# A shorter list of warm-up matmuls ahead of a weight-gradient matmul

## Chip, core and metric

The kernel runs on one core of one Trainium2 chip. The metric is device time in microseconds (us), as the median of several executions. Next to these timed runs there is one profiled execution with a trace; its times are counted from the first instruction of its span.

## What is computed

```python
def setup_inputs():
    batch, m, k, n = 16, 512, 1024, 768
    return {
        "input": np.random.randn(batch, m, k).astype(np.float32),
        "grad_output": np.random.randn(batch, m, n).astype(np.float32),
    }

def reference(input, grad_output):
    return np.einsum('bmk,bmn->kn', input, grad_output).astype(np.float32)
```

The batch and m axes are summed over together, so this is one matmul: an X of 8192 x 1024, transposed, times a G of 8192 x 768, which gives 1024 x 768 in fp32. Both inputs come from HBM as fp32 and are multiplied as bf16.

## The kernel before

**Tiles.** The 8192 rows are cut into 32 units of 256 rows. A unit is a pair of tiles, `xp` (128 partitions x 2 x 1024) and `gp` (128 x 2 x 768), in bf16. `LOADS` gives each unit a kind: the first five and the last are "s" (multiplied plainly, as two row tiles of 128), the other 26 are "P". For a "P" unit VectorE (DVE) first makes sums and differences of its quarters into `xe` and `ge` (`sum_x` and `sum_g`, lines 202 to 220), and TensorE then does seven products of quarters in place of eight.

**Loads.** The first row tile's G and the first two row tiles' X come as fp32 (`gf`, `xf`) through the queues of SyncE and ScalarE (lines 150 to 153), and are rounded to bf16 by DVE and ScalarE (ACT) in line 224. Everything else comes through GpSimd's (POOL's) queue, which rounds on the way: lines 180 and 182 for single row tiles, then lines 175 and 176 for whole units, G first and then X. Transfers are issued in this order far ahead of their use; a later one waits for a free buffer of the pool `pairs`.

**Warm-up.** Before the first data is there, TensorE (PE) multiplies constants into one PSUM bank that nobody reads before it is overwritten. The list `WARMUP` (line 88) names these matmuls, and the loop in lines 155 to 164 issues them; the profile puts them at line 158. They read constants of 1.0 that lie in SBUF from the start, so they wait for no load. All the real matmuls have line 328 (`multiply`).

**Order.** `PLAN` (lines 24 to 85) is a list written out by hand: each token is a multiplication of a block for some row tiles, a filling of a bank with a running sum (line 302, ACT), a closing of a bank (lines 355 to 371), a set-aside (383), an adding of what was set aside (392) or a stage of the sums. The order on PE, DVE, ACT and POOL is that of the program and is not rescheduled. So an instruction that waits holds up all that stands behind it on its engine.

**Instructions.** Each real matmul is two instructions on PE, a weight load and a multiplication, and so is each bf16 warm-up matmul. PE's instructions are brought in while the kernel runs, by transfers that use the same 16 DMA engines as the loads; the page lists them as "q8 instruction".

Of the kernel before, what the change touches and what calls it, by code (L numbers as in the profile page):

```python
# [9 lines left out]
P = 128  # L10
# [74 lines left out]
).split()  # L85


WARMUP = [("b", 512)] + [("s", 80)] * 54
PAIRS_HELD = 10
SUMS_HELD = 8  # L90
ASIDE = 24
# [18 lines left out]
def kernel(  # L110
# [6 lines left out]
    nc = tc.nc  # L117
    bf16 = mybir.dt.bfloat16
    f32 = mybir.dt.float32
# [34 lines left out]

    wps = psum.tile([P, 512], f32, name="bank7")
    for dt, cols in WARMUP:
        rows = 32 if dt == "s" else P
        nc.tensor.matmul(
            wps[0:rows, 0:cols],
            nc.const_aps.tensor(1.0, (P, rows), bf16),  # L160
            nc.const_aps.tensor(1.0, (P, cols), bf16),
            start=True,
            stop=True,
        )
# [4 lines left out]
    for u, kind in enumerate(LOADS):  # L169
# [3 lines left out]
        if u >= MERGED:  # L173
            rows = slice(2 * u * P, 2 * (u + 1) * P)
            nc.gpsimd.dma_start(out=gp, in_=G[rows, :].rearrange("(p m) n -> p m n", m=2))  # L175
            nc.gpsimd.dma_start(out=xp, in_=X[rows, :].rearrange("(p m) k -> p m k", m=2))  # L176
        for h in range(2):
            s = 2 * u + h
# [222 lines left out]
    for token in PLAN:  # L401
# [6 lines left out]
        elif op == "f":  # L408
            block, banks = rest.split("@")
            b, _, b2 = banks.partition("+")  # L410
# [9 lines left out]
        else:  # L420
            block, n = token.split(".")
            block, _, banks = block.partition("@")
            b, _, b2 = banks.partition("+")
# [33 lines left out]
```

## Time and profile before

| what | value |
|---|---|
| timed runs | 161.83, 161.84, 162.16 us; median 161.84 |
| profiled execution | span 160.0 us, 1.84 less than that median |
| PE | 155.1 us busy (97%), 1057 matmuls, of which 55 are the warm-up |
| DVE | 146.8 us busy (92%) |
| ACT / POOL | 118.2 us (74%) / 39.6 us (25%) |
| the 16 DMA engines | 33.42 MB in 12447 packets, "9" in nearly all slices up to the 35th of 40 |
| PE's instruction transfers (q8) | 8 packets, 0.13 MB |
| HBM | 58.72 MB read, 3.15 MB written |

"Busy" is an engine's own time with an instruction on it; PEld is the loading of weights, which overlaps multiplication. The page gives no time of the profiled execution besides its span, so what lies around the span is taken as the 1.84 us to the median. A slice is a fortieth of the span, 4 us. A wait is put down to what released it.

### The profile page before, as it was taken

The page shows a single profiled execution, that of the slowest core. Times are in us where ns is not written, and L with a number is a line of the kernel's source. Part 1 is how long each engine was busy: PE and PEld are TensorE (multiplying, and loading weights), DVE is VectorE, ACT ScalarE, POOL GpSimd, SP SyncE. Part 2 cuts the span into 40 slices and gives each one's busy share as a digit, 9 for nine tenths or more (in the row PEclk, how much of TensorE's full clock was granted, in tenths as well). Part 3 has the DMA queues.
Part 4 walks back from the last instruction along what each step waited for, and adds up shares of the span by engine and source line. Part 5 has one row for each costly group of instructions (what it writes and reads, how often), then busy time and mean ns, then how long its engine had stood idle before and what let it go on. Part 6 is the DMA issues. An engine that isn't in the chain of part 4 may idle for free.

```text
span 160.0 us, 3074 instructions
## 1 busy us (share of the span) xinstructions
PE 155.1 (97%) x1057; PEld 98.4 (62%) x1057; DVE 146.8 (92%) x344; ACT 118.2 (74%) x274; POOL 39.6 (25%) x74
## 2 busy tenths in 40 slices
PE   8999899999999999999999999999999999999991
PEld 7666476666666666666656666666666666656661
DVE  0689979999999999999999999999999989998991
ACT  3683444899788788988986596985789855685960
POOL 7442222122221222222122221222222100004510
PEclk9999999999999999999999999999999999999999
DMA  5999999999999999999999999999999999931786
GB/s 174 298 211 215 212 216 213 211 215 212 212 213 213 212 211 213 213 214 214 216 215 213 212 211 214 212 213 210 212 217 212 212 215 215 212 64 45 218 294 234
DMA packets 12447, 33.42 MB, mean 209 GB/s; under 512 B 1424, under 2 KB 4240, under 8 KB 12432
## 3 DMA queue, kind: packets, MB, share of 16 engines
q0 software_dynamic: 9360, 28.64, 90.5%
q1 hardware_dynamic: 2640, 3.41, 6.6%
q10 hardware_dynamic: 432, 1.18, 2.0%
q8 instruction: 8, 0.13, 0.3%
q14 instruction: 7, 0.06, 0.1%
HBM read 58.72 MB, written 3.15 MB: 387 GB/s over the span
## 4 chain that ended last, share of the span: by engine, by line
PE 85%; DMA 8%; POOL 2%; ACT 1%; issue 1%; DVE 1%; ACTq 0%; POOLq 0%
PE bank L328 85%; DMA xp<-in_input_dram 8%; POOL gp L180 1%; POOL xp L182 1%; ACT bank L302 1%; ACT acc L367 1%; DVE acc L369 1%; POOL gp L175 0%; ACT macc L367 0%; ACTq L367 0%; POOLq L441 0%
## 5 line engine op out<-in xcount | busy, mean ns | idle before, releaser
L328 PE MATMUL bank<-gp,xp 128*128 128x384 bf16 (+2 forms) x690 | 109.1, 308 | 0.8 <-DMA xp<-in_input_dram 0.5
L328 PEld LDWEIGHTS <-xp 128*128 128x128 bf16 x690 | 64.6, 98 | 37.9 <-DMA xp<-in_input_dram 0.8
L328 PE MATMUL bank<-ge,xe 128*128 128x384 bf16 x312 | 59.7, 326 | 0.0
L328 PEld LDWEIGHTS <-xe 128*128 128x128 bf16 x312 | 30.3, 98 | 19.0
L302 ACT COPY bank<-macc 128x384 f32<-128x384 f32 x73 | 34.4, 486 | 7.0 <-DVE macc L371 2.5
L367 ACT COPY macc<-bank 128x384 f32<-128x384 f32 x68 | 31.4, 482 | 5.7 <-PE bank L328 5.0
L176 POOL DMA_DIRECT2D xp<-in_input_dram x30 | 15.9, 529 | 53.0 <-DVE ge L218 21.0
L367 ACT COPY acc<-bank 128x384 f32<-128x384 f32 (+1 forms) x39 | 18.3, 477 | 12.3 <-PE bank L328 12.2
L175 POOL DMA_DIRECT2D gp<-in_grad_output_dram x30 | 15.9, 531 | 37.4 <-DMA gp<-in_grad_output_dram 10.4
L371 DVE TENSOR_TENSOR acc<-bank,acc 128x384 f32<-128x384 f32 x45 | 23.7, 555 | 0.6 <-PE bank L328 0.4
L302 ACT COPY bank<-acc 128x384 f32<-128x384 f32 (+2 forms) x45 | 20.9, 480 | 4.3 <-DVE acc L371 1.9
L383 ACT COPY aside<-bank 128x384 f32<-128x384 f32 x43 | 19.1, 483 | 6.0 <-PE bank L328 5.1
L371 DVE TENSOR_TENSOR macc<-bank,macc 128x384 f32<-128x384 f32 x38 | 21.2, 558 | 0.6 <-PE bank L328 0.5
L206 DVE TENSOR_TENSOR xe<-xp 128x1024 bf16<-128x1024 bf16 x26 | 18.0, 692 | 0.0
L392 DVE TENSOR_TENSOR acc<-acc,aside 128x384 f32<-128x384 f32 x26 | 14.5, 556 | 1.3 <-ACT aside L383 1.3
L216 DVE TENSOR_TENSOR ge<-gp 128x768 bf16<-128x768 bf16 x26 | 14.5, 558 | 0.0
L392 DVE TENSOR_TENSOR macc<-macc,aside 128x384 f32<-128x384 f32 x20 | 11.2, 563 | 0.0
L210 DVE TENSOR_TENSOR xp<-xp,xe 128x512 bf16<-128x512 bf16 x26 | 11.0, 425 | 0.1
L208 DVE TENSOR_TENSOR xe<-xe,xp 128x512 bf16<-128x512 bf16 x26 | 11.0, 424 | 0.1
L399 POOL TENSOR_TENSOR acc<-acc,macc 128x384 f32<-128x384 f32 x5 | 5.0, 1000 | 21.6 <-DVE macc L364 19.7
L220 DVE TENSOR_TENSOR gp<-ge,gp 128x384 bf16<-128x384 bf16 x26 | 9.3, 358 | 0.1
L218 DVE TENSOR_TENSOR ge<-gp,ge 128x384 bf16<-128x384 bf16 x26 | 9.3, 359 | 0.0
(20 smaller groups left out, 42.7 us busy)
## 6 DMA issues: line engine op xcount, KB each, us to landing
xp<-in_input_dram POOLq DMA_DIRECT2D x30, 512.0 KB, 16.9
gp<-in_grad_output_dram POOLq DMA_DIRECT2D x30, 384.0 KB, 16.8
out_dram<-acc SPq DMA_DIRECT2D x12, 192.0 KB, 2.0
xf<-in_input_dram ACTq DMA_DIRECT2D x2, 512.0 KB, 5.0
gp<-in_grad_output_dram POOLq DMA_DIRECT2D x3, 192.0 KB, 6.4
out_dram<-acc SPq DMA_DIRECT2D x6, 96.0 KB, 2.2
xp<-in_input_dram POOLq DMA_DIRECT2D x2, 256.0 KB, 7.8
gf<-in_grad_output_dram SPq DMA_DIRECT2D x2, 192.0 KB, 4.4
```

Source lines behind the costliest of these rows:

```text
L175: nc.gpsimd.dma_start(out=gp, in_=G[rows, :].rearrange("(p m) n -> p m n", m=2))
L176: nc.gpsimd.dma_start(out=xp, in_=X[rows, :].rearrange("(p m) k -> p m k", m=2))
L206: nc.vector.tensor_sub(out=xe[:, 0:2, :], in0=x[:, 1::-1, :], in1=x[:, 3::-2, :])
L208: nc.vector.tensor_sub(out=xe[:, 2, :], in0=xe[:, 0, :], in1=x[:, 0, :])
L210: nc.vector.tensor_add(out=x[:, 1, :], in0=x[:, 2, :], in1=xe[:, 2, :])
L216: nc.vector.tensor_add(out=ge[:, 0:2, :], in0=g[:, 0:2, :], in1=g[:, 1::2, :])
L302: nc.scalar.copy(out=tile_[:, t0 : t0 + c1 - c0], in_=sum_of(p, q)[:, c0:c1])
L328: nc.tensor.matmul(tile_[:, t0 : t0 + c1 - c0], stat, mov[:, c0:c1], start=start, stop=True, skip_group_check=True,)
L367: nc.scalar.copy(out=d, in_=b)
L371: nc.vector.tensor_add(out=d, in0=b, in1=d)
L383: copy(out=aside[i], in_=b[:, t0 : t0 + NH])
L392: nc.vector.tensor_add(out=dst, in0=dst, in1=aside[i])
```

## The change

```diff
-WARMUP = [("b", 512)] + [("s", 80)] * 54
+WARMUP = [("b", 512), ("f", 512), ("f", 512), ("b", 512)]
...
     for dt, cols in WARMUP:
-        rows = 32 if dt == "s" else P
+        kind = f32 if dt == "f" else bf16
         nc.tensor.matmul(
-            wps[0:rows, 0:cols],
-            nc.const_aps.tensor(1.0, (P, rows), bf16),
-            nc.const_aps.tensor(1.0, (P, cols), bf16),
+            wps[:, 0:cols],
+            nc.const_aps.tensor(1.0, (P, P), kind),
+            nc.const_aps.tensor(1.0, (P, cols), kind),
```

Before, the warm-up is one bf16 matmul of 128 x 128 weights and 512 columns, and then 54 of 128 x 32 weights and 80 columns. After, it is a bf16 one of 512 columns, two fp32 ones of 512 columns and again a bf16 one, all with 128 x 128 weights. In the program's own list an fp32 matmul is one instruction (it loads its weights itself), so 110 instructions become 6, 104 fewer. In the compiled stream of PE each fp32 matmul is two pairs of a load and a multiplication, one for each of two parts of the weights, so 110 become 12, 98 fewer. On DVE, ACT, POOL and SyncE the instructions and their order stay as they are, and on PE everything behind the warm-up does too.

## The prediction

> **What bounds the kernel now.** First the page, for who is busy and who waits.
>
> ```profile
> span 160.0 us, 3074 instructions
> ...
> PE 155.1 (97%) x1057; PEld 98.4 (62%) x1057; DVE 146.8 (92%) x344; ACT 118.2 (74%) x274; POOL 39.6 (25%) x74
> ...
> L328 PE MATMUL bank<-gp,xp 128*128 128x384 bf16 (+2 forms) x690 | 109.1, 308 | 0.8 <-DMA xp<-in_input_dram 0.5
> ```
>
> TensorE is busy all but 5 us, and all its real matmuls together waited 0.8 us. So only the start, the end and that one wait can move the time through TensorE. Next the chain of work that ended last, in order of time, for where that wait lies.
>
> ```profile
> 4.05 0.48 POOL gp L175
> 4.53 12.36 DMA xp<-in_input_dram
> 16.89 0.05 issue
> 16.93 62.51 PE bank L328 x417
> ...
> 82.28 74.04 PE bank L328 x490
> ```
>
> The columns are start, length and what. Up to 16.89 the end is set by a load, the X of the third unit; from 16.93 on by TensorE, to 156.3. How fast TensorE starts matters only as far as it reaches 16.93 late. Then TensorE's first microseconds in the timeline, and equal stretches of it in the view by windows (stretch; its length; PE's busy time and matmuls; then the other engines, clock, DMA).
>
> ```profile
> 0.78 4.29 PE L158 MATMUL bank<-const-bfloat16-1.0 128*128 128x512 bf16 x55 [0.78 <-PEq L441]
> 5.29 2.98 PE L328 MATMUL bank<-gp,xp 128*128 128x256 bf16 x16 [0.22 <-ACT xp L224]
> ```
>
> ```profile
> 5.30:6.40 1.10, 1.10 (x5) 0.67 (x6) 0.37 (x2) 0.24 (x1) 0.33 (x1) 1.00 1.08 298
> 6.40:7.50 1.10, 1.10 (x10) 0.69 (x8) 1.03 (x5) 1.03 (x3) 0.00 (x0) 1.00 1.16 207
> ...
> 16.45:16.95 0.50, 0.04 (x2) 0.02 (x2) 0.50 (x2) 0.48 (x1) 0.00 (x0) 1.00 1.15 227
> ```
>
> The warm-up ends 0.2 us before the first real matmul, which waits for ACT's rounding. In the 1.1 us before 6.40 TensorE does 5 matmuls, in the 1.1 us after it 10: its clock comes to full pace at 6.40 only. The 1.00 that the page prints before that is not a measurement: the trace's own clock record begins at 6.40. And in the third stretch TensorE stands still. Last, the DMA view around 13 us.
>
> ```profile
> q0 software_dynamic: 62, 0.24, 100.5%
> q8 instruction: 1, 0.02, 4.9%
> ```
>
> Between 13.2 and 14.4 us, while the loads fill all 16 DMA engines, one of them carries a packet of TensorE's instructions: in the packet records 16384 bytes, at 13.33, for 0.945 us. The landing records say what it costs. The awaited X comes in 16 pieces, one for each engine: 15 land between 15.59 and 16.16, and the last at 16.89. The transfer before it has no such straggler (13.14 to 13.69), and all later ones have: unit four's X lands by 20.51 in 15 pieces, the last at 21.20. So **the wait at 16.9 is made by the instruction packet**, which put one engine 0.73 us behind for good, as it is never idle.
>
> **The change part by part.** *Instructions.* The eight q8 packets begin when 215, 504, 722, 986, 1238, 1497, 1747 and 1955 of TensorE's records have started: one for about 249 (1955 less 215, by 7). They go by count. With 98 fewer ahead of them (104 in the program's list), the first comes at the old record 313 to 319, at 21.5 to 21.9 us, less what TensorE has gained: about 21. By then X of units three and four is in. Unit three's X then lands at 16.16 instead of 16.89, and TensorE, 0.04 behind it as now, can go on at 16.20 instead of 16.93: at most **-0.73 us**.
>
> *The warm-up's length.* TensorE is ready for that X at 16.31 now (its last matmul before started at 16.15, and they are 0.163 apart). That is after it lost half of 5.29 to 6.40 to the slow clock, 0.555 us. So the new restart is the later of 16.20 and 16.31 + (new loss - 0.555). A bf16 matmul of 512 columns takes 0.51 (0.78 to 1.29, where the next starts). No row shows an fp32 one. From below: as bf16, 0.51 each, so the warm-up ends at 0.78 + 4 x 0.51 = 2.8. From above: DVE's bf16 add of 1024 columns takes 692 ns and its fp32 add of 384 takes 556, so 0.68 and 1.45 ns a column, 2.14 times; both operands are wide here, so 4.6 times 0.51, 2.35 each, and the end is at 6.5. The compiled stream has two multiplications for each, so I stay near the upper end with 1.9: 0.78 + 0.51 + 3.8 + 0.51 = 5.6. The first real matmul then starts 0.31 late. With the clock at full pace from 6.40 again, the loss is 0.31 + 0.40 = 0.71, TensorE is ready at 16.47, and -0.46 is left. With an end at 5.29 it is -0.62; where the clock comes by 5.8 it is the full -0.73. One execution does not tell where between these the clock falls, so I take **-0.6**. The Trainium skill, "FP8 and Floating Point Precision", TensorE Precision Notes, gives true fp32 four passes through the array; at the slow pace of 0.43 us for 512 columns that would be an estimate of 1.7 each, and the sum would be -0.62.
>
> *What is hidden.* Going 0.6 earlier, TensorE and DVE need every later load 0.6 earlier, and the DMA engines are full until about 140, so those land where they do now. Between landing and use there are now 0.13 us at unit four's X (21.20 to 21.33), but there the straggler goes too: 15 pieces are in by 20.51, the need is at 20.7. After that X is used on TensorE 0.63 us or more after landing (the least at 139.06 and 143.46, with 0.63 and 0.73). On DVE it is 0.59 at 37.3 and 0.46 to 0.52 at 130.5, 134.6 and 138.9, so DVE may stand up to 0.15 there; its own idle gaps of 0.33 at 142.1 and 0.71 at 145.3 take that back. Cost 0; with that cover gone, 0.15. The other instruction packets come some 8 us later too; one that meets the engine furthest behind just ahead of 139 costs up to 0.6. The 0.26 us that TensorE stands at 81.9 for DVE and ACT moves along; should it vanish, that is the low end.
>
> *Sum.* 160.0 - 0.6 = 159.4 of span, and with the 1.84 between this span and the median, **161.24**. Its own range: 161.84 - 0.73 - 0.26 = 160.85 to 161.5.
>
> **The rivals.** *The instruction transfer was hidden, or the wait comes back.* If the straggler has another cause, X still lands at 16.89. Or TensorE's stream asks for its instructions 1 us sooner than I count, and the packet delays unit four's X: it lands at 21.20 again, where TensorE then stands 0.5. Either way 161.7 to 161.84. For it: 0.13 us of margin is little, and the packets' spacing varies from 208 to 289 records. Against: 15 of 16 pieces were early, from the transfer that was on its way at 13.33 on and on none before. The Trainium skill, "Runtime: Kernel Launch", Instruction fetch mechanics, calls the cost of crossing such a 16 KiB block mostly hidden; by that rule nothing would change, but the 0.73 us of the late piece speaks against it.
>
> *The clock comes later.* If the fp32 matmuls end early, or count less for the clock, TensorE runs its real matmuls at half pace for longer. The loss is half of (opening - 5.29). It decides once it is 0.555 + 0.626 = 1.18 (16.93 less 16.31 is the 0.626), so for an opening after 7.65. Before, the clock came 5.62 us after TensorE began; if only real matmuls counted, it would come at 5.29 + 5.62 = 10.9, with a loss of 2.81: ready at 18.57 and 163.5. The middle of 7.65 and 10.9 is 9.3: loss 2.0, +0.82, **162.7**. For it: no row shows an fp32 matmul, and one as quick as bf16 would leave TensorE idle from 2.8 to 5.29. Against: the small matmuls before filled only 32 columns of the array and still opened the clock. The Trainium skill, "TensorE: Matmul & The Clock Gate", HAM clock gate, has the clock decided in free-running windows of 3.41 us; one window late would be 9.81, an estimate of 162.9.
>
> *The warm-up is simply too long.* Past 2.35 us for an fp32 matmul the first real one starts after 6.5; each 0.1 us more costs 0.2. At 2.6 each the end is at 7.0, the loss 1.71, and the time 162.4. Only wider operands than the rows suggest would do that.
>
> **How the numbers follow.** Forecast 0.62, hidden or returned 0.16, clock later 0.17, too long 0.05. Within 0.2% (0.32 us) is what a measurement of this kernel can't tell from no change. Nearly all of the forecast's cases lie beyond it: faster 0.62, same 0.17, slower 0.21. The range goes from 160.8, with the stall at 81.9 gone, to 162.6, which takes in the second case, the third and the near half of the clock's; about 0.1 lies above.
>
> **What would show it.** Right: the first q8 packet near 21 us, and no piece of unit three's X late; TensorE's wait for it gone or under 0.1; TensorE's last matmul 0.5 to 0.7 earlier than 156.4. The fp32 step: the first real matmul between 5.29 and 5.6. Wrong: a full clock later than 7.65 (few matmuls between 6.4 and 7.5), a wait at 21, or a new one at 139.

## The result and the profile after

| | before | after |
|---|---|---|
| timed runs | 161.83 to 162.16, median 161.84 | 162.42 to 162.84, median 162.75 |
| ratio after to before | | 1.0042, 95% interval 1.003 to 1.0054 |
| span of the profiled execution | 160.0 | 161.1 (that execution took 162.84) |
| last matmul on PE starts | 156.43 | 156.08 |
| from there to the end of the span | 3.55 | 4.98 |

The change makes the kernel 0.9 us slower by the medians and 0.7 by the ratio, where 0.6 us faster was forecast. It did bring TensorE forward, though by 0.34 us only; then the end, from the start of TensorE's last matmul on, became 1.43 us longer (4.98 against 3.55). The difference of the two, 1.09, is that of the spans. The profiled execution is the slowest of the change's five (the others have spans of 160.5 to 161.0), so the 1.43 is at the upper end of what was lost, if TensorE gained as much in them.

First the page of the kernel after, the lines that answer to those shown of before.

```profile
span 161.1 us, 2976 instructions
...
PE 155.3 (96%) x1008; PEld 95.8 (59%) x1008; DVE 146.7 (91%) x344; ACT 118.3 (73%) x274; POOL 39.8 (25%) x74
...
L328 PE MATMUL bank<-gp,xp 128*128 128x384 bf16 (+2 forms) x690 | 109.2, 307 | 0.2
```

The engines' work is what it was. In the last line the wait for a load is gone: 0.8 us of idle time has become 0.2, and no load is named as its releaser. Next TensorE's first microseconds in the timeline, and two stretches in the view by windows (the same columns as before).

```profile
0.78 0.58 PE L158 MATMUL bank<-const-bfloat16-1.0 128*128 128x512 bf16 x1 [0.78 <-PEq L441]
1.16 3.62 PE L158 MATMUL bank<-const-float32-1.0 128*128 128x512 f32 x4
4.57 0.63 PE L158 MATMUL bank<-const-bfloat16-1.0 128*128 128x512 bf16 x1
5.22 2.96 PE L328 MATMUL bank<-gp,xp 128*128 128x256 bf16 x18
```

```profile
5.30:6.40 1.10, 1.10 (x9) 0.67 (x10) 0.65 (x3) 0.54 (x2) 0.34 (x1) 1.00 1.10 302
...
16.45:16.95 0.50, 0.39 (x3) 0.12 (x2) 0.50 (x2) 0.35 (x1) 0.50 (x1) 1.00 1.08 215
```

The warm-up ends in time: the first real matmul starts at 5.22, and in the 1.1 us from 5.30 TensorE does 9 matmuls where it did 5 before, so its clock is up earlier (the clock record begins, at full, at 5.48; before at 6.40). At 16.45, where it stood still before, it works 0.39 of 0.50 us. The chain of work that ended last says what holds it up there instead.

```profile
5.22 7.23 PE bank L328 x45
...
13.88 2.88 DVE acc L371 x6
16.76 0.04 issue
16.81 58.25 PE bank L328 x390
...
81.94 74.04 PE bank L328 x490
155.98 0.02 issue
156.00 0.02 ACTq L367
156.02 0.04 issue
156.06 0.38 ACT acc L367
156.44 0.29 DVE acc L369
```

Where the chain before had a load of 12.36 us, it now has a run of six of DVE's additions, until 16.76. The matmul that waited for the load starts at 16.20 (16.93 before), so the whole 0.73 is won there. But then TensorE stands 0.27 us behind the matmul of 16.37 and 0.14 behind that of 16.97, for banks that DVE has still to empty. So the load no longer decides, and DVE does: 0.34 is left of the gain, at 81.94 (82.28 before) as at the end.

The chain stops at the end of DVE's last copy, at 156.73, and says nothing of the 4.3 us behind it, in which the results are stored. These lines are of the DMA view of before, from 144.0 to 145.4 us, and then of after, from 152.3 to 154.3.

```profile
DMA packets 1, 0.02 MB, mean 12 GB/s; under 512 B 0, under 2 KB 0, under 8 KB 0
...
q8 instruction: 1, 0.02, 6.2%
```

```profile
q1 hardware_dynamic: 138, 0.19, 26.8%
q8 instruction: 1, 0.02, 4.5%
```

TensorE's last instruction packet (the eighth) came at 144.20 before, when all loads were in and no store was under way: it was the only packet in 1.4 us. In the kernel after it comes at 152.45, among the output stores (q1). What the stores do around it is in SyncE's timeline (start, time to issue; the eleventh of the 20 stores, before, then after) and in the windows (the last two columns are the DMA engines' busy share and GB/s; before, then after).

```profile
152.69 0.38 SPq L346 DMA_DIRECT2D out_dram<-acc  x1
```

```profile
152.34 1.93 SPq L346 DMA_DIRECT2D out_dram<-acc  x1
```

```profile
152.00:153.00 1.00, 1.00 (x8) 0.60 (x7) 1.00 (x4) 0.80 (x3) 0.67 (x1) 1.00 0.39 140
153.00:154.00 1.00, 1.00 (x8) 0.59 (x6) 1.00 (x3) 1.00 (x3) 0.00 (x0) 1.00 0.90 326
154.00:155.00 1.00, 1.00 (x8) 0.59 (x6) 1.00 (x3) 0.60 (x3) 0.00 (x0) 1.00 0.97 346
155.00:156.00 1.00, 1.00 (x10) 0.76 (x8) 1.00 (x3) 0.00 (x0) 0.00 (x0) 1.00 1.03 369
```

```profile
152.00:153.00 1.00, 1.00 (x8) 0.59 (x6) 1.00 (x4) 0.80 (x3) 0.33 (x1) 1.00 0.35 109
153.00:154.00 1.00, 1.00 (x8) 0.59 (x6) 1.00 (x4) 1.00 (x4) 0.00 (x0) 1.00 0.31 109
154.00:155.00 1.00, 1.00 (x9) 0.60 (x7) 1.00 (x3) 0.26 (x2) 0.00 (x0) 1.00 0.26 91
155.00:156.00 1.00, 1.00 (x12) 0.87 (x11) 0.98 (x2) 0.00 (x0) 0.00 (x0) 1.00 1.03 369
```

The store that meets the packet takes 1.93 us to issue, until 154.27, and until it is done SyncE issues no other. Of the store ahead of it, issued at 151.92, 15 of the 16 pieces are in by 153.77 in the landing records, and the last at 155.24: one engine is behind. The DMA view from 153.5 to 154.5 us says what the others do meanwhile (packets, MB, share of 16 engines; before, then after).

```profile
q1 hardware_dynamic: 270, 0.37, 101.7%
```

```profile
q1 hardware_dynamic: 4, 0.01, 4.1%
```

The 4.1% are less than a sixteenth, the share of one engine at work. So the other 15 stand, until the next store is issued and its packets begin. From 152 to 155 the DMA engines work 0.92 us (0.35 + 0.31 + 0.26) where they worked 2.26 before: 1.34 us of all 16 engines are lost. They can't be made up: from 155 on the stores go at 364 to 369 GB/s in both kernels, one of 192 KB each 0.54 us, nearly to their end. The last store's transfer ends at 158.72 before and at 159.80 after, 1.08 later, as the span does.

### The profile page after: what moved, and what is told of

The parts are those of the page before. It is cut to its first block, busy times and chain, and to the rows that moved or that the text cites. A ratio compares the mean times of both kernels' runs of the same rounds, so it can differ in the third digit from the quotient of the medians.

```text
span 161.1 us, 2976 instructions
## 1 busy us (share of the span) xinstructions
PE 155.3 (96%) x1008; PEld 95.8 (59%) x1008; DVE 146.7 (91%) x344; ACT 118.3 (73%) x274; POOL 39.8 (25%) x74
## 3 DMA queue, kind: packets, MB, share of 16 engines
q1 hardware_dynamic: 2640, 3.41, 6.6%
## 4 chain that ended last, share of the span: by engine, by line
PE 89%; ACT 3%; DVE 3%; issue 1%; ACTq 0%
PE bank L328 87%; PE bank L158 3%; DVE acc L371 2%; ACT bank L302 1%; ACT macc L367 1%; ACT acc L367 1%; DVE acc L369 1%; ACTq L367 0%
## 5 line engine op out<-in xcount | busy, mean ns | idle before, releaser
L371 DVE TENSOR_TENSOR macc<-bank,macc 128x384 f32<-128x384 f32 x38 | 20.9, 551 | 0.6 <-PE bank L328 0.5
```

Of the source, the lines that this page charges most:

```text
L371: nc.vector.tensor_add(out=d, in0=b, in1=d)
```

## The experiments

The theory: the place of the instruction packets decides, both at the loads and at the stores, and that place follows from the number of instructions ahead of them on TensorE. Its rivals: the fp32 warm-up matmuls themselves, or the fullness of SyncE's queue. Each run has another warm-up list, or another queue for some stores, or both. The table gives the PE instructions of the warm-up, when the first and the last packet begin, when X of unit three is complete, when TensorE's last matmul starts, what follows from there to the span's end (the tail), the DMA share from 152 to 155 us, the median, and the ratio to the kernel before on the same chip. The medians are of more than one chip, so kernels are compared by the ratio.

| kernel | instr. | first | X three | last | PE last | tail | share | median | ratio (95%) |
|---|---|---|---|---|---|---|---|---|---|
| before | 110 | 13.33 | 16.89 | 144.20 | 156.43 | 3.55 | 0.75 | 161.84 | 1 |
| after | 12 | 21.36 | 16.15 | 152.45 | 156.08 | 5.0 | 0.31 | 162.75 | 1.0042 (1.003 to 1.0054) |
| e1 | 40 | 18.78 | 16.23 | 150.70 | 156.39 | 4.0 | 0.69 | 162.03 | 1.0002 (0.9992 to 1.0012) |
| e2 | 20 | 21.14 | 16.14 | 152.31 | 156.21 | 4.4 | 0.49 | 162.35 | 1.0029 (1.0018 to 1.004) |
| e3 | 40, fp32 | 18.57 | 16.14 | 150.61 | 156.24 | 3.9 | 0.76 | 161.95 | 1.000 (0.999 to 1.001) |
| e4 | 80 | 15.81 | 16.16 | 146.44 | 156.27 | 3.6 | 0.82 | 161.65 | 0.9988 (0.9976 to 1.0) |
| e5 | 268 | 8.03 | 17.20 | 153.19 | 156.74 | 5.0 | 0.44 | 163.32 | 1.0071 (1.0046 to 1.0096) |
| e8 | 96 | 14.51 | 17.17 | 145.96 | 156.70 | 3.5 | 0.76 | 161.88 | 0.9996 (0.9986 to 1.0005) |
| e9, after + ACT stores | 12 | 21.53 | 16.42 | 152.73 | 156.26 | 4.7 | 0.46 | 162.51 | 1.0029 (1.0016 to 1.0041) |
| e10, before + ACT stores | 110 | 13.45 | 17.00 | 144.46 | 156.54 | 3.5 | 0.75 | 162.07 | 1.0004 (0.9996 to 1.0013) |
| e11, e4 + ACT stores | 80 | 16.2 | 16.39 | 146.24 | 156.51 | 3.6 | 1.03 | 161.78 | 0.9996 (0.9985 to 1.0008) |
| e12, e2 + ACT stores | 20 | 20.7 | 16.22 | 152.19 | 156.06 | 4.5 | 0.48 | 162.34 | 1.0028 (1.0019 to 1.0037) |

**bf16 warm-ups of another count.** Each of e1, e2 and e4 starts from the kernel before and takes another list, without fp32; the second number of a pair is the columns of that matmul.

```diff
-WARMUP = [("b", 512)] + [("s", 80)] * 54
+WARMUP = [("b", 512)] + [("s", 227)] * 19   # e1
+WARMUP = [("b", 490)] * 10                  # e2
+WARMUP = [("b", 512)] + [("s", 111)] * 39   # e4
```

> Warm-up: one bf16 matmul of 512 columns and 19 small ones (32 weight columns, 227 columns), as long as before at the slow clock, with 40 instructions (70 fewer than before; the changed kernel has 98 fewer). Theory 'packets': the time follows from where TensorE's instruction packets fall. Here the first should come near 21.0 us, after the X of unit four has landed, and the eighth near 150.1 us, where SyncE's store queue still waits 1 us for its data. So TensorE gains about 0.35 as in the changed kernel and the end loses nothing: span 159.6 to 159.8, time about 161.5, faster than before by 0.3 and than the changed kernel by 1.2. Rival 'warm-up': the changed kernel is slow since 54 small matmuls are gone (clock, fp32). This one has small ones again, so it expects 161.84 as before. Rival 'fewer instructions cost as such': about two thirds of the loss, 162.4.

> Warm-up: ten bf16 matmuls of 490 columns, no fp32, as long as the others at the slow clock, 20 instructions (90 fewer than before). Theory 'packets': first packet near 21 us (TensorE gains 0.35), the eighth near 151.8 us, in the row of stores: one store is issued 1.5 us late and those behind it with it. Span near 160.7 to 161.1, time 162.4 to 162.8, like the changed kernel though nothing in it is fp32. Rival 'fp32': without fp32 the loss is gone, 161.5 to 161.84.

> Warm-up: one bf16 matmul of 512 columns and 39 small ones of 111 columns, 80 instructions (30 fewer than before). Theory 'packets': the first packet can't be asked for before the wait for unit three's X is over, so it comes near 16.7 us; unit three's X is on time (16.16), but unit four's X is then 0.7 late (21.2), and TensorE stands there 0.2 to 0.5. Eighth packet near 146.7, harmless. Time 161.7 to 161.84: the gain of the first wait is given back at the second. If it were enough to have the first packet off unit three's X, the time would be 161.5.

e2 has no fp32 matmul and the packets where the change has them. It loses too, 1.0029 against 1.0042, and the loss lies in the same place: 4.4 us from TensorE's last matmul on. e1 missed what was expected of it, 161.5. Its first packet comes at 18.78 and makes unit four's X late (21.42, against 20.50 in the change), though TensorE does not wait there; its last one still meets a store, at 150.70. TensorE's last matmul is only 0.04 earlier than before, as in this execution TensorE also stood 0.44 us at 6.79, for a rounding by DVE. e4 has both packets in places that cost little, 15.81 and 146.44, and has the lowest ratio of all. Its windows:

```profile
152.00:153.00 1.00, 1.00 (x8) 0.60 (x7) 1.00 (x3) 0.79 (x3) 0.50 (x1) 1.00 0.45 163
153.00:154.00 1.00, 1.00 (x8) 0.59 (x6) 1.00 (x3) 1.00 (x4) 0.00 (x0) 1.00 1.01 363
154.00:155.00 1.00, 1.00 (x8) 0.59 (x6) 1.00 (x3) 0.44 (x2) 0.00 (x0) 1.00 0.99 353
```

No hole here, and 3.6 us to the end, as before. So a part of the first gain can be had by itself: 0.16 us at TensorE's last matmul, as here the packet delays X of unit four (21.29, and TensorE stands 0.26 at 20.9). The interval touches 1.

**fp32 alone, at a held count.** e3 has the change's two fp32 matmuls, and 15 small ones of 16 columns, with 32 weight columns as in the kernel before, that bring the count to e1's 40.

```diff
-WARMUP = [("b", 512), ("f", 512), ("f", 512), ("b", 512)]
+WARMUP = [("b", 512), ("f", 512), ("f", 512)] + [("s", 16)] * 15
```

> Warm-up: one bf16 and two fp32 matmuls of 512 columns as in the change, then 15 of 16 columns in place of the last bf16 one: 40 instructions (70 fewer than before). Theory 'packets': first packet near 21.0, eighth near 150.1, time about 161.5, the same as with 40 instructions in bf16 alone. Rival 'fp32': the fp32 matmuls stay, so the loss stays, 162.4 to 162.8.

e3 and e1 agree in time (161.95 and 162.03, intervals that overlap), in the first packet (18.57 and 18.78), in the last (150.61 and 150.70) and in the tail (3.9 and 4.0). Like e1 it misses the 161.5 that was expected. e2 has the loss without fp32, and e3 has fp32 without most of the loss: fp32 is not the cause. This is e3's store at its last packet, in SyncE's timeline:

```profile
150.63 1.67 SPq L347 DMA_DIRECT2D out_dram<-acc  x1
```

It takes 1.67 us to issue, 1.76 in e1. A store of 1.35 to 1.93 us stands beside the last packet in each of the kernels where it comes between 150.6 and 153.2 (after, e1, e2, e3, e5, e6, e9, e12). Where it begins by 146.5 (before, e4, e8, e10, e11), none from 152 to 156 takes over 0.40.

**More instructions, not fewer.** e5 has 268 warm-up instructions. If the packets go by blocks of 256, it is 12 plus one block, and the change's loss comes back with a longer list; if fewer instructions were the cause, it goes the other way. e8, with 96, leaves the first packet within X's transfer.

```diff
-WARMUP = [("b", 512)] + [("s", 80)] * 54
+WARMUP = [("b", 512)] + [("s", 36)] * 133   # e5
+WARMUP = [("b", 512)] + [("s", 92)] * 47    # e8
```

> Warm-up: one bf16 matmul of 512 columns and 133 small ones of 36 columns, as long as before, with 268 instructions, 158 more than before. As a packet comes for every 256 instructions, this is the changed kernel's pattern (98 fewer) with one packet more, early in the warm-up. Theory 'packets, counted modulo 256': a first one at 3 to 5 us, which leaves one DMA engine 0.7 us behind before the first unit has landed, then one near 21.5 and the ninth near 152.5, in the row of stores, with 1.0 to 1.5 us lost at the end. Time 163.0 to 163.8, slower than before by more than the change was. Rival 'fewer instructions are what costs': more instructions than before would be no slower, 161.84 to 162.0.

> Warm-up: one bf16 matmul of 512 columns and 47 small ones of 92 columns, 96 instructions, 14 fewer than before. Theory 'packets': the first packet comes near 14.5 us, still while unit three's X is on its way, so that lands 0.7 late as before; the eighth near 145.4, harmless. 161.84 to 162.0, as before. If it were each instruction saved that counts, a seventh of the change's loss, or with 30 fewer a gain of 0.2: 161.7 to 162.0, not to be told apart; so the trace decides: the X of unit three late (over 16.8) by the theory, on time (16.2) if the shift needed is smaller.

In e5 the packets come at 8.03, at 22.00 (the change's 21.36) and, as the ninth, at 153.19 (152.45). It has the same tail of 5.0 us, and the load wait besides; of all kernels with the stores left on their queues it is the slowest. The waits of TensorE (total, times, longest), in e5 and then in e8:

```profile
PE bank L329 <- DMA xp<-in_input_dram: 0.9, 2, 0.6
```

```profile
PE bank L329 <- DMA xp<-in_input_dram: 0.8, 1, 0.8
```

An early packet (8.03, and 14.51 in e8) makes X of unit three late, 17.20 and 17.17, and the wait is there. A packet after X's pieces are under way, as e4's at 15.81, leaves it at 16.16. The Trainium skill, "Runtime: NRT & Kernel Launch", Instruction fetch mechanics, says that the instructions of an engine come in 16 KiB blocks of 256 and that the cost of crossing a block is mostly hidden. The blocks agree with the packets' size here and with e5. The cost does not: 0.73 us at a load, and the 1.43 us at the end.

**Stores through POOL's queue.** If SyncE's full queue were the harm, stores on another queue would pass the stuck one. e6 is the change, and e7 the kernel before, each with three late stores on POOL's queue.

```diff
             stored.append(rows)
+            if queue is nc.sync and len(stored) in (12, 14, 16):
+                queue = nc.gpsimd
```

(In the kernels the two new lines stand ahead of the append.)

> The changed kernel, with 3 of its 19 late stores on SyncE's queue (the 13th, 15th and 17th) moved to POOL's queue, which is empty from 152.3 us. Theory 'the eighth packet holds up SyncE's store queue': one store is still issued 1.5 us late near 152.4, but SyncE then has 3 stores fewer behind it, some 0.5 us each, and catches up. Time between TensorE's last matmul and the end goes from 5.0 us to 3.6 to 4.0; TensorE's gain of 0.34 shows: 161.5 to 161.9. Rival 'the end is long for another reason' (the transfers themselves slow): nothing changes, 162.4 to 162.8.

> The kernel before with the same 3 stores moved to POOL's queue: the control. No packet falls in its stores (the eighth is at 144.2 us), SyncE's queue is only 0.5 us or less behind its data, so nothing to win: 161.7 to 161.9. If it gains as much as the changed kernel does by it, the gain is not about the packet.

Both are slower than anything else: 164.44 (ratio 1.0156, 1.0137 to 1.0175) and 164.97 (1.0184, 1.0166 to 1.0202). Here the last data lands at 159.84 and 160.20, but POOL, once it has issued such stores, is done only 2.1 and 2.3 us after that (161.90 and 162.54), where the kernel after waits 0.2 for it. Nor can POOL's stores fill the hole: the first is issued at 153.78 in e6, but its first packet starts 1.57 us later, at 155.35, and in e7, without an instruction packet among the stores, it is 1.55. So the pair can't tell the queue's share. In it the change is the faster one, by 0.53: the end hangs on POOL's last store, which is issued as soon as its data is there, at 155.69 in e6 and 156.33 in e7. That is the distance of TensorE's last matmuls, 156.04 and 156.68; a part of it is chance, as TensorE in e7 also stood 0.54 us at 6.7 for a rounding.

**Stores through ScalarE's queue.** e9 to e12 put two late stores, the 15th and the 16th, on ACT's queue, in the change, in before, in e4 and in e2.

```diff
+            if len(stored) in (14, 15):
+                queue = nc.scalar
             stored.append(rows)
```

> The changed kernel with two of SyncE's late stores (the 15th and 16th) on ScalarE's queue, which is idle from 154.3 to 156.1 us; no store goes through POOL. Theory 'the eighth packet holds up SyncE's queue': SyncE still issues one store late near 152.4, but has two fewer behind it and is back at its data by the last ones. From TensorE's last matmul to the end of the span 3.8 to 4.2 us in place of 5.0; time 161.6 to 162.0, 0.8 to 1.1 below the changed kernel. Rival 'the end is long for another reason': 162.4 to 162.8 as it is.

> The kernel before with the same two stores on ScalarE's queue, the control: no packet falls in its stores, 161.7 to 162.0, within 0.1 of before. With e9 it gives the change with the store queue relieved: theory 'packets' has the change 0 to 0.35 faster there, where it was 0.4% slower.

> The warm-up of 80 instructions (e4) with the same two stores on ScalarE's queue. Its eighth packet comes before the stores, so by the theory the relief is worth 0 to 0.1: 161.5 to 161.7.

> The warm-up of ten bf16 matmuls (e2, 20 instructions) with the same two stores on ScalarE's queue. Eighth packet near 152.3, TensorE's gain 0.2: theory 'packets' 161.6 to 161.9 in place of 162.35; rival 162.35 as in e2.

e10 shows that the edit itself costs nothing that can be measured. e9 and e12 missed: 162.51 and 162.34, where the gain was expected to come through. The windows of e9 show the hole again.

```profile
153.00:154.00 1.00, 1.00 (x8) 0.59 (x6) 1.00 (x3) 1.00 (x4) 0.00 (x0) 1.00 0.94 338
154.00:155.00 1.00, 1.00 (x8) 0.59 (x6) 1.00 (x3) 0.44 (x2) 0.00 (x0) 1.00 0.07 15
155.00:156.00 1.00, 1.00 (x11) 0.80 (x9) 1.00 (x3) 0.00 (x0) 0.00 (x0) 1.00 0.78 283
```

The hole comes with the packet, here at 152.73, and is deepest from 154 on: 0.07. SyncE's store at 153.16, the twelfth, takes 1.58 us, until 154.74; ACT issues its two at 154.72 and 155.20 with 0.38 and 0.41, and behind them SyncE's are slow again (0.60, 0.93 and 0.82 at 155.80, 156.49 and 157.51). The last store's transfer ends at 159.74, 0.06 before the change's. But ACT issued its stores when their data was there (at 155.00 and 155.47 in e10, whose TensorE is 0.28 later), and that was when the stuck issue ended. The 13th and the 14th, whose data was there by about 153.7 and 154.2 (e10 issues them at 154.01 and 154.48), still stood behind the stuck one. So whether a second queue would have brought stores past it, e9 and e12 do not show; this rival stays open. The Trainium skill, "Trainium Kernel Development and Optimization", Key Constraints, says that all these queues run on the same 16 DMA engines and that issuing from several saves only the sequencer's time. For the full engines behind the hole e9 agrees: from 156 to 158 SyncE's and ACT's queues together move 366 GB/s, and SyncE's alone moves 369 and 366 there in before.

e11 shows the other side. Its last packet, at 146.24, meets a store too, which takes 1.39 us to issue. But there the stores are sparse (a DMA share of 0.25 from 146 to 148 and of 0.47 from 148 to 150), and the engines catch up: 1.03 from 152 to 155, the last transfer done at 158.81 (158.82 in e10), the tail 3.6. So it is not the slow store that costs, but transfer time lost where the engines have none left. The tails follow the shares of the table: those of 4.4 to 5.0 us have 0.31 to 0.49. Only e1 and e3, with 4.0 and 3.9, lose theirs partly ahead of that stretch, as their packet comes at 150.7 and 150.6: from 150 to 152 their share is 0.79 and 0.76, and before's is 0.85.

## Why the prediction was wrong

- **The first packet: right.** It was put near 21 and comes at 21.36. X of unit three is complete at 16.15 (16.16 forecast), and unit four's at 20.50 (20.51). e5 and e8, with an early packet, have the late X and the wait, 17.20 and 17.17; e1 to e4 have neither. That the straggler is made by the packet is shown. That its engine then stays behind "for good" was too much: in before the last piece is 0.69 to 0.74 behind the others in the next three transfers of X, and 0.30 and 0.11 in the two after them, at 34.14 and 38.56.
- **The warm-up: right, and mis-sized to the good.** The four fp32 multiplications start 0.853 us apart, so a matmul costs 1.71, where I took 1.9. The first real matmul starts at 5.22 rather than by 5.6, and the clock is up at 5.48. The rivals of a late clock and of a long warm-up did not come about. That the first named a time of 162.7 is chance: its mechanism needs an opening after 7.65.
- **The size of the gain: -0.6 forecast, -0.34 measured.** I took TensorE to be ready at 16.31 and after that to wait for nothing. It was ready by 16.20, and had the full 0.73 there; it then waits for DVE, 0.27 and 0.14 us. I checked DVE only against its loads (0.15 of standing at most), not whether it would empty TensorE's banks 0.6 us earlier. In no kernel is TensorE's last matmul more than 0.39 earlier (156.04 in e6). That DVE is the reason is read from the chain; no run took work off DVE.
- **"What is hidden": the step that failed.** It said that "the other instruction packets come some 8 us later too", and then asked only which loads they meet: "one that meets the engine furthest behind just ahead of 139 costs up to 0.6". The seventh comes at 136.41 and costs nothing that the trace shows. The eighth, at 144.20 before, was the one to look at: 8 us on from there is 152, in the middle of the stores, which in the windows of before fill 0.90 to 1.03 of the engines from 153 on. It cost 1.43 us, some four times the gain that was left. The sum had no term for it, so the range ended at 162.6, below the 162.75 measured.
- **Not in question:** the absolute times of the later loads did not move (the last X lands at 142.72 in both), as forecast.

What stays open: why a store's issue lasts so long beside a packet on one engine, and whether stores on another queue, with their data there, would have kept the other 15 engines at work. That the packet does it is shown by where it goes, in the two kernels and the ten runs whose end does not hang on POOL; taking the eighth packet out altogether was not tried. No version is clearly faster than the kernel before: e4, with 0.12%, has an interval that reaches 1.

## What to carry to other kernels

Instructions are data too: a changed count ahead of a long stream moves every later instruction transfer, so follow each of them, the last above all, to what it will meet there, loads and stores alike. A gain at one wait is worth only what the next engine in line lets through. And the end of this kernel, where nothing was left to make lost transfer time up, was the dearest place for a disturbance; the chain of waits, which stopped at the last copy, does not show it.

## What was not expected of the hardware

- The last packet took 1.385 us at 144.20 in before, where it was the only packet in the engines, and 1.15 to 1.64 among the stores, but 0.945 at 145.96 in e8, ahead of the stores, and 0.89 to 1.08 among the loads. So its length isn't a matter of the traffic around it alone.
- While the engines are full, the one that carried a packet stays behind through several transfers: in before X of unit three has its last piece 0.73 after the others, and the next three X have theirs 0.69 to 0.74 after.
- The time at which the clock record becomes full varies from 3.75 us (e11) to 6.51 (e3), with no order by the kind of warm-up. The Trainium skill, "TensorE: Matmul & The Clock Gate", HAM clock gate, has windows of 3.41 us that run freely, and a spread of 2.76 fits within one of them.
- An fp32 multiplication of 512 columns takes 0.853 us ahead of the start of the clock record. In e2 the ten bf16 ones of 490 columns, ahead of it too, take 4.24 us, 0.42 each, so an fp32 one is two of them, and a matmul, with two multiplications, four. That agrees with the four passes that the prediction quoted.
